# Low parts of 22 weight blocks: a GpSimd subtraction, or an accumulating DMA onto a negated copy

## The chip, the core and the metric

The kernel runs on one core of a Trainium2 chip. The metric is the device time of one execution in microseconds (us). TensorE (PE, with its weight loads PEld) does the matrix products, VectorE (DVE), ScalarE (ACT) and GpSimd (POOL) the rest; SyncE (SP) issues the DMAs of the kernel before. Line numbers such as L427 are those of the kernel's file; since every instruction is issued from one line of a recording helper, the names of tiles tell instructions apart.

## The reference

One decoder layer over x of 1024 tokens by 1024 channels, in float32, with a modulation vector c:

```python
mod = silu(c) @ w_mod + b_mod                    # sh1, sc1, g1, sh2, sc2, g2
h = rms_norm(x, norm_mix_w) * (1 + sc1) + sh1
proj = h @ w_in                                  # 1024 x 3080
x_lru, y_lru, qkv, z, beta, alpha = split(proj)  # 512, 512, 3 x 512, 512, 4, 4
out_lru = rms_norm(rg_lru(conv(x_lru), ...) * gelu(y_lru), lru_norm_w)
q, k, v = silu(conv(qkv))                        # 4 heads of 128
o = gated_delta_rule_chunked(q, k, v, g, beta)
out_gdn = rms_norm(o, gdn_norm_w) * silu(z)
x = x + g1 * (concat(out_lru, out_gdn) @ w_out)
h = rms_norm(x, norm_mlp_w) * (1 + sc2) + sh2
x = x + g2 * (square(relu(h @ w_up)) @ w_down)
out = rms_norm(x, final_norm_w)
```

The delta rule needs, for each chunk of a head, the inverse of a triangular matrix made from k, beta and g.

## The kernel before

**Two parts for each operand.** A product in float32 is made of three products in the faster type fp32r: an operand is split into a high part (the value rounded to fp32r) and a low part (the value minus the high part), and `mm3` adds high x high, high x low and low x high in one PSUM bank. Its third matmul is the one that reads the low part of the weights.

**The input projection.** `w_in` is worked off in 24 blocks of 128 columns (`Proj`): k0 to k3, z0 to z3, then q and v of each of four heads in turn, then lx and ly of four channel tiles in turn. `Proj.split` loads a block of 1024 x 128 as a tile of 128 x 1024 (512 KB), casts it on ScalarE to its high part (`k_wh`, `z_wh` and so on) and subtracts to get its low part (`k_wl`, `z_wl`). For k0 and k1 the subtraction is on VectorE, for the other 22 blocks on GpSimd. `Proj.third` makes the product for 342 of the columns of h at a time (the last two of 1026 carry a bias): 8 x 3 matmuls of 342 columns, so 72 for a block. ScalarE then evicts the three results (`k_st`, `z_st`).

**What hangs on a block.** `key(h)` takes a projected k through a convolution and silu (`k2T`, `k3T`: one ScalarE multiplication, three VectorE steps, one ScalarE tanh `k2th`, `k3th`, one VectorE step), transposes it on TensorE (`ktok`), multiplies it with itself (`kk`), scales with `rnk` (a power on GpSimd), `bcoef` and the decay (`k_dm`) and writes `LT`. After k3, `inverse` runs a long row of small VectorE steps (`ftmp`, `xx`), transposes the result (`xnc`, `xtc`), copies it to `xn` and `xt`, and multiplies on TensorE (`ie`, `ig`, `ih`, `ix`). Then come query, value and the chain over the chunks (`ch`), the RG-LRU (`lru`), the output projection (`wg`, `wl`), and the MLP as a seven-product Strassen scheme (`upx`, `upy`, `upz`, `dn`).

**The order.** Nothing is issued while the kernel is written down. A `Recorder` collects every operation with a planned duration, and `schedule` simulates the five engines and puts their instructions in an order that is then fixed. The large products are a backbone (`bb`) with due times from a backward pass; other operations get the due time of what needs them, moved by one entry of the table `SHIFTS` for each operation. On an engine, a ready side operation goes ahead of the backbone. The backward pass is

```python
for op in reversed(ops):
    op.lst = min((ops[j].lst - lat(op, ops[j]) for j in op.succs), default=0.0) - op.dur * scale(op)
```

Large tiles, the raw block and both of its parts among them, share a pool of 43 buffers; a buffer comes free when the last operation that uses its tile has ended. The planner lets only one of GpSimd and some VectorE instructions run at a time (`port`).

Of the kernel before, what the change touches and what calls it, by code (L numbers as in the profile page):

```python
# [51 lines left out]
LOAD_WINDOW, DUE = 40.0, 5.0  # L52
RESERVE = {"b": 11, "ps": 2, "u": 1, "c": 2}
# [67 lines left out]
def dram_box(ap):  # L121
# [7 lines left out]
    'c-qaId2m(NeaC<AJ?ZI5LLdnV0RkZwiG4R<wm^)7YrMprIwncm)J@}Qn;B2s&a}-;-8P+MlCeAWA6YtW)=nmlGmY(z3C0fC21AT77@NiHn8ip4f%'  # L129
    'X-NC;j^Qo%_IG`(AS%vFr1jyS#hvx%Zsk`7Phy@0^#`w7v|jSNWjw&9C+Kw%f@gO~HjJheRg#*x5f{vi-x<OUf<RRC=f{IG#@j$BiBGF_eaG+uxu'  # L130
    '0_O5~3b>G0Eo_FtW8hH2o?GNZ}bLLu6`uV|I2Oq!m-usK({d=@J9o>#ro%nn2TN|U~Tjz`hBr-xS>2PV$J)AF+Cp1UWdXn=AvOzcNo4S+p<+4r>>'
    'JBZW=2VGGLP|vScKMQ|ptuytP<iOeyG!JI@<94#*(2j*TY9S``wv_^qcQ2=dxP4?`w|%*$N08LF27ZW(gu-Q$&nr{<=Z<{KGCHgZWuq-$QNZmUx5'
    'c>>3N9^anz>?dL=SODr7p8lqK>xxHO<m@}~UTd)}p2`uZeWySBrDv~H1IaQ?JTme0sy$<Mtd_p$h9_+xZJFKLHX@XadOEL-Gv@`ko(z0Tr`9eT-|'
    'cSor4XrfN5V>!~K)ux~NliYl%=KJkh<oeWsZ1n3{MzJ2cpc_*!Cvs%Cl*&jcW-Qmnb|)su&GhEH7Sr$JT1k&9C11u%4Zn@XaMq|J<Q<*HHk!@1rI'
    'qxwRR`$%zc&6%zI0(jU4DJlz}4eY%rke$47n94Kcq*IxM?z5=DE=+N5X_(CdKW%C8#q<or&xR>8b6FVw^Q;5{<2+$31YjO;78AETpnL_o#QR@!nt'
    'Q)^42{uZG8QYWHg#&CHcv#_S&Sdba$D%;H|I6lC<R2dj~$P9@S*A#;$?2iT8fw5s6Wbe^tdtmZIc(>b%+2{_uVWpWCB_Aqvpa#-hiw{s#gwNlE@`'
    'qgUDb)G!@Pd%r3GFzwWEBcRm99#CfdqV@VYvbFFlrN`mWyo$L<D7&?v(dEAprc8+P|B8%jKtWRv=zx*s9$@L{B68*DEt++el@v@!|4u3J=f47-Ks'
    'C>(>lt1B`8DC+NA8%X7r#6%A*~(@V$x93N-yLEX5l66fG-*!#i)#4i>Pj&TMPg9*|!k5#Qnb5p2>^Tz`V?VaDX!+?^w%XwfKISS|DE^DLPxeR|nS'
    'T~8Tw{Z6A>X?i#SHF8ZeT4nNM?;nX}DCM1bP?1M(hC9lpd<}XU64{Pjt&=v+_R3G>Tk<co=iBl_`0)s5tB`_G@1t>!mNP!99NmuePj)mP9<7zn%A'
    'K;1^F`2DSs?duoQn^gBa>u3GUQ*1y=(MlfdX#IQmS4;vOgX_o5xoFv3#rB`zwLO$E3@<rs=(JX;=RmlR;Sh;DJhxLmbXftXmw*lFvRLlu?ddk2!z'  # L140
    'PPhXlq9)noMGBnh;tU!}jde>_Dy^QT5S%wDA$MY?A`a1;6JOrPgkh6HgVyJ*Vn#Vh=$8@hYfN|^Ta~IT)jf(O7B`pwtO|_96^zOrq8`6k?;%pPKq'
    'NSPN1GK+|{^a3Z&S@t-9n5HHuWm;Mj>CyI&6m%EX*TI=YB9~DVllu9d0g+sBitcV<iB(V=;#}|R$tYx>oa<CFb-$x^@y4TT~eb)e5*LW5cq}`H8O'
    '-BT)E7}BxiMS`?&rVOEbk?>GS5*7)Sp2+_y#&?wB;@aBjXoh)|j|#n#|R9HxKQ7sVW<z(++$!91wS`OjI5%V#+o&lpwEk^otnt;nG#39jXUMDwXt'
    '!d3&#1OeP8ce5?xdBfWYFurdOEHa3DbLyww-`Ni@{z8U1gxm}sDnh~(Evf_26w3u&jCXw7#W0HG+yh$7rT0tOa*_OTaBL>g!BTY6Xt;FhDJ)beR;'
    'K{2-6h|UAK*b%S2?8Gr?qb1rnfjAp3pBMwS~kED;TqRvOG2lsoH^bzk}=-$fx1pEN53@a5;xjZ3VCW2T{qdiC$XuCF<rn{qg73AUbx3cdb@$4yTD'
    'o&eP&^IvxobCWfO5ke!mN#=2WCG7cuErlEyARVbsO5l|Vwn&Cz-*HtT=Or_vP%=Ozlg5hm(Nq^*Cm?#%n=%%k{>HBo9SZq0(Z6<9fC$?NbuRq18j'
    '{%DfMbFOZGWHgoKC4?8<>Oeb9=$jApzPA;^ygTr(Xv&)A`c>U+x0~!bK^ncH-X$lw$P)a$mBLQqs<(@!tt5RZ?k7#kO0ZYi5vzv#^8kgE_YJ)XW;'
    'a&y9j?6^j)}nj0mAiE$4NY8^@T#;InC=$&Iyi8rm@zYdDpw6KH)GeeKGEx975`<3EO_$W{)$G;i_8Qt0>+lwq9pX+Wj$B*m2qIM9bj?MF6~V#k6^'
    'b|atbCeb6rte|BX-cWzPS?n~>w~WFj`PC@G`o=)?DP%9@`f60-EWJgLUzXPyxeG2+l9D}eBF3GQ`f#k$dEXR0Ol3ysIlVkm2Q~1N_Qo={B@Q*+iN'
    'zARHxr+&0maOx?ouRnDPLR)eV*e3Y+sg}h$t>P*}I$8CD4OD{WS7a$-9=I_bai7_u@qk;H9li1M1uJo6wI6Zw}XZ*RVLd-(?{EN~g}wB9`(+9ix!'  # L150
# [23 lines left out]
    '#<|Y#)#B?c5?`E!oYgx7T_D*+2DaLyl5J!bU%pKyyA@ld;;&bOaKYyHS|W2BVKGWl#!IKur;ju1Q0lC95_!n;u3P4^bmOu4e-5w5Va;qdvl02&s}'
    '&&a!}x|%>OTWB#H|)G?{*ws`txHi(L}r2+*`E_Wbyw#TZNT$`SPS27vFOE|0_E)|K`YMTukn>%~o{L`;9~wo6yf4H~3$`Gg+)MvXyJ*opRjF_io*'
    ')+w_gA;)Lrhdo-Y}VAcb=J&P42bBKedIeazR*=)b^j2ebor_bwhEUv%3T+R2(@iHaI;Uu?S%~u9enYHfaj{ZMN;)>r-WKnmlL#x5wsL0Xit0?#%k'
    'd?`qE7_GJE>H1{K8|1Vt-DjdhlCwvoR59NbHwk@78Yeut6fhz#NVC;&bI%<*i6JJ9qRqvAg&DJ_UUXRu&s;m8@6V1j@#SO(3u?rX{g9rBCahqM=$'
    '|y#qce@C5TbaYc^}%>#uOy-;X4(p~WC&qvddCnEQ|6WeWZs?7xb%BJ*bBOL@fnV7MGLWpX=p;PIbju{yd8|I(-p*cQtl`qrP4q1r2F{|BmuXWI')
SHIFTS = array.array("h", zlib.decompress(base64.b85decode(_SHIFTS))) if _SHIFTS else None
# [1500 lines left out]
```

## Time and profile before

| | us |
|---|---|
| median of 3 runs | 1164.97 (1164.01 to 1165.21) |
| profiled execution, first to last instruction (span) | 1162.6 |
| what lies around the span, against the median | 2.4 |
| PE busy | 1137.1 |
| POOL busy | 371.4, 221 instructions |
| ACT busy | 616.5 |
| DVE busy | 834.6 |

The record of the profiled execution gives its span; its time is compared with the median through the 2.4 us of the third row. Busy time is the union of an engine's instructions. A matmul is pipelined: its row gives some 320 ns for a 342-column one, though in an unbroken row the next one starts earlier. In a timeline a line has the start, the length, the engine, operation and tiles, and in brackets how long the engine stood idle before it and what ended that. A row of a group has busy time, the mean of one in ns, and the idle time before, with its releasers.

### The profile page before, as it was taken

What the parts mean: (1) busy time and instruction counts of PE and PEld (TensorE: products, weight loads), DVE (VectorE), ACT (ScalarE), POOL (GpSimd) and SP (SyncE); (2) the same over time, 40 slices, a digit from 0 to 9 for tenths busy, and PEclk for the clock granted to TensorE, in tenths of its full rate; (3) what the DMA queues carried; (4) which work ended last, traced back from release to release, by engine and by line L of the source; (5) the groups of instructions that cost most, each with busy time, mean ns of one, the idle gap of its engine ahead of it and who ended that gap; (6) DMA issues with size and microseconds to landing.
All of it is one profiled execution on the core that took longest, in us unless ns stands there. A gap on an engine that the chain in (4) does not pass through costs nothing.

```text
span 1162.6 us, 15986 instructions
## 1 busy us (share of the span) xinstructions
PE 1137.1 (98%) x5952; PEld 979.8 (84%) x5952; DVE 834.6 (72%) x1123; ACT 616.5 (53%) x988; POOL 371.4 (32%) x221
## 2 busy tenths in 40 slices
PE   6899999999999999999999999999999999999997
PEld 3799999999999998887888888887888888888885
DVE  5778786687986879778776776766885583865563
ACT  5547445445547866477655555556644533363441
POOL 1329512253424463300003231311450057723030
PEclk9999999999999999999999999999999999999999
DMA  9623432544454462422276887773999956864541
GB/s 338 223 86 110 134 121 75 180 121 159 152 185 145 135 230 107 145 84 80 65 267 237 274 281 247 252 244 136 364 403 388 369 175 247 308 226 168 199 163 72
DMA packets 127151, 229.52 MB, mean 197 GB/s; under 512 B 10657, under 2 KB 51806, under 8 KB 127074
## 3 DMA queue, kind: packets, MB, share of 16 engines
q1 hardware_dynamic: 127074, 228.51, 56.7%
q8 instruction: 46, 0.75, 0.3%
q14 instruction: 31, 0.25, 0.1%
HBM read 171.83 MB, written 56.65 MB: 197 GB/s over the span
## 4 chain that ended last, share of the span: by engine, by line
PE 91%; DMA 3%; DVE 3%; ACT 1%; issue 1%; SPq 1%; POOL 0%; POOLq 0%; ACTq 0%
PE dn L427 26%; PE upx L427 15%; PE upz L427 8%; PE wg L427 4%; PE upy L427 4%; PE wl L427 4%; PE z_p L427 4%; PE lx_p L427 4%; PE q_p L427 4%; PE ly_p L427 4%; PE v_p L427 3%; PE k_p L427 2%; PE ch L427 2%; SPq L427 1%; DMA sh_w<-in_w_mod_dram 1%
## 5 line engine op out<-in xcount | busy, mean ns | idle before, releaser
L427 PE MATMUL upx<-h2h,U 128*128 128x512 f32 x512 | 168.0, 394 | 0.0
L427 POOL TENSOR_TENSOR wd<-wd,wd 128x512 f32<-128x512 f32 x32 | 49.9, 1568 | 214.4 <-DMA wd<-in_w_down_dram 163.4
L427 PEld LDWEIGHTS upx<-h2h,U 128*128 128x128 f32 x512 | 96.0, 188 | 22.5
L427 PE MATMUL upx<-h2l,U 128*128 128x512 f32 x256 | 100.8, 394 | 0.0
L427 DVE TENSOR_TENSOR U<-wu,U 128x512 fp32r<-128x512 f32 x112 | 85.0, 774 | 18.1 <-ACT U L427 17.9
L427 ACT ACTIVATE act<-act 128x512 f32<-128x512 f32 x112 | 70.3, 632 | 44.9 <-DVE act L427 43.2
L427 PE MATMUL upz<-h2h,U 128*128 128x512 f32 x256 | 85.0, 394 | 0.0
L427 ACT CAST U<-wu 128x512 fp32r<-128x512 f32 x112 | 66.8, 617 | 27.8 <-DVE wu L427 10.0
L427 PEld LDWEIGHTS upx<-h2l,U 128*128 128x128 f32 x256 | 48.1, 188 | 11.5
L427 PEld LDWEIGHTS upz<-h2h,U 128*128 128x128 f32 x256 | 48.1, 188 | 11.4
L427 DVE TENSOR_TENSOR act<-upz,ek 128x512 f32<-128x512 f32 x32 | 22.1, 690 | 40.1 <-PE upz L427 25.9
L427 ACT COPY ek<-upx 128x512 f32<-128x512 f32 x48 | 28.0, 584 | 42.6 <-PE upx L427 42.4
L427 PE MATMUL upz<-h2l,U 128*128 128x512 f32 x128 | 50.4, 394 | 0.0
L427 POOL TENSOR_TENSOR R<-R,R_5o 128x1024 f32<-128x1024 f32 x8 | 20.0, 2520 | 74.4 <-DMA R<-in_w_down_dram 63.2
L427 PE MATMUL upy<-h2h,U 128*128 128x512 f32 x128 | 42.7, 394 | 0.0
L427 POOL TENSOR_TENSOR ssq<-ssq,mhalf 128x1 f32<-128x1 f32 x16 | 11.6, 725 | 84.8 <-DVE ssq L427 84.8
L427 DVE TENSOR_TENSOR wu<-wu,wu 128x512 f32<-128x512 f32 x48 | 36.1, 759 | 0.5 <-DMA wu<-in_w_up_dram 0.4
L427 ACT ACTIVATE vn<-ch,bcoef 128x128 f32<-128x128 f32 x32 | 11.8, 368 | 45.0 <-PE ch L427 44.9
L427 PE MATMUL k_p<-hh,k_wh 128*128 128x342 f32 x96 | 31.9, 332 | 1.0 <-ACT hh L427 1.0
L427 PE MATMUL k_p<-hl,k_wh 128*128 128x342 f32 x96 | 32.0, 333 | 0.8 <-DVE hl L427 0.8
L427 PE MATMUL k_p<-hh,k_wl 128*128 128x342 f32 x96 | 31.9, 332 | 0.0
L427 PE MATMUL ly_p<-hh,ly_wh 128*128 128x342 f32 x96 | 31.7, 330 | 0.0
(574 smaller groups left out, 3719.3 us busy)
## 6 DMA issues: line engine op xcount, KB each, us to landing
L<-aod SPq DMA_DIRECT2D x56, 512.0 KB, 6.5
R<-in_w_down_dram SPq DMA_DIRECT2D x40, 512.0 KB, 5.9
wu<-in_w_up_dram SPq DMA_DIRECT2D x32, 512.0 KB, 5.0
aod<-as SPq DMA_DIRECT2D x64, 256.0 KB, 3.3
wd<-in_w_down_dram SPq DMA_DIRECT2D x32, 512.0 KB, 6.5
aod<-act SPq DMA_DIRECT2D x48, 256.0 KB, 2.9
x<-in_x_dram SPq DMA_DIRECT2D x16, 512.0 KB, 4.6
sc_w<-in_w_mod_dram SPq DMA_DIRECT2D x16, 512.0 KB, 7.2
```

The source lines that it names most:

```text
L427: op.fn(*[res(v) for v in op.a], **{n: res(v) for n, v in op.k.items()})
```

## The change

For the 22 blocks, ScalarE writes the negated high part into the low part's tile, and a DMA issued by GpSimd adds the raw block to it in place. The planner learns of such an operation: 1.1 us of GpSimd, and a landing time after it that delays those who need the result. `SHIFTS` is another table, so the order of instructions differs on all engines. k0 and k1 keep their subtraction on VectorE.

```diff
+ADD_ISSUE, ADD_LAND, ADD_RATE = 1.1, 2.5, 150e3
...
 _SHIFTS = (
...
-        op.adj = SHIFTS[len(self.ops)] / 4.0 if SHIFTS else 0.0
+        op.adj = SHIFTS[len(self.ops)] / 4.0 if SHIFTS and len(self.ops) < len(SHIFTS) else 0.0
...
                 now[e] = fin = t + (clock.run(t, op.dur, op.work) if e == "PE" else op.dur)
                 port = max(port, fin) if op.port else port
+                fin += op.tail
...
+class Adder(Proxy):
+    def __getattr__(self, name):
+        fn = getattr(self.nce, name)
+
+        def call(out, in_):
+            n = 4
+            for d in out.shape:
+                n *= d
+            self.rec.add("POOL", fn, (), {"out": out, "in_": in_, "accum_op": ALU.add}, [out], [in_, out], ADD_ISSUE)
+            self.rec.ops[-1].tail = ADD_LAND + n / ADD_RATE
+        return call
...
+    GD = Adder(rec, "POOL", nc.gpsimd)
...
             A.copy(self.w[0], raw)
-            e.tensor_tensor(out=self.w[1], in0=raw, in1=self.w[0].bitcast(F32), op=ALU.subtract)
+            if e is G:
+                A.mul(self.w[1], self.w[0].bitcast(F32), -1.0)
+                GD.dma_start(out=self.w[1].bitcast(F32), in_=raw)
+            else:
+                e.tensor_tensor(out=self.w[1], in0=raw, in1=self.w[0].bitcast(F32), op=ALU.subtract)
```

More of the change, by code (lines that the diff above doesn't have):

```diff
@@ L134 @@
[L134 to L138, printed above, removed]
@@ L174 @@
[L174 to L178, printed above, removed]
+    'c-qZd2XIy8x?SHsCkc?y5(q><AoQk4ODNI}AXS<mNQ)v$lPW|EO%PDQ!j(`(lxE@5L<FvaC`~|0gosojNJ2t@bdsF!u6?*O_stvsGqW>qoVPP4=Vb5wx'
@@ new lines @@
+    '38>kt$&|XhoG9LvhGm))iHN`ZuUL<!@`t@Cu*MuYGv7<V)N|ZGc;Q#=}L|NAMIbwefXZ7|L}d!ef$l_pPBaWVgDKX=YlSJrXV8gzt{H`{P**vzgTVRf6'
+    'f)p-|gw>S)cd6uSa;V_tGl)zUNUMBmU3V_JZfW$7!2z{G{Qip`|ermvyi1)C^sKE?9tBSfbOg5%KyJ@^qQrMxf+rHyw)~wUgXMUmUb%y3e}?Nrc2=wJT'
+    'Qq(aJi3auRHPCM!{0YKljP=Xb{jl$4S(8)Z;ml0DZ8N@1Gz&{FtR1F%}>X;19bdwNBC>KYxTA7Bzf&|B})k`=A`IHLG}ew49_Ksn3BNJBT-hVQW&FUcL'
+    'Nwlqdd3`0F$U5$ZqU;R;AB5@jFvIP@l5yokvZh}AR>La+RG5V6eg|4y!pUd-zlc9LZO4Wf#L@=h%CI^v(9D3+HuIYBIAV26$6$D|IK8h_`4Mk}25E-cj'
+    '`aaJW!ABb9*mlR*;t%$jhAdA$BjK!W&|v>${YWdp#jCIANZv6)&w5_x7|D#5C*X$w&g%*~NHlJtEN2JQKqMNV1j^xUJdIVdQuat4v_XHlEX(DZOhzoGv'
@@ new lines @@
+    ';B77`#@FKI*#05^pMuX&ukyZxT(z5PEU;X=Ijp5(F1x~lhp-}rg((5%i#H7apAmrbO0uzKjxtwLZvz0!}B<-osp=4II0tA>#MpFosg*~*}gfEZ!6yi75'
+    'u2sg}BX3N!8i9ME5ziZ8mLm$8mK1?s%NCIHlj}B-;LS4dwh(^&93_hQ7;dop21lc=P@_#37F>KEeo%l1<F-3t9sAG*i>`HqRboq;)_(^Yo-VkeZCiHF9'
+    '1oS}TY>Dz@unscL0uG>XX%&C<pg<#?ukjEw><d(&B~@3GzCNC!2aEfNsp`An<mc|EGPbS^sMJ4ST?(zOnIoPuwdiDgh(M&pDQ!zk30T&aj(HH`ON(XSX'
+    'uZ|EZC*-p4zi4tK&%W=G+!_W->VlM2|K^!R#hqSI0g|Y182IKl3d$O}CU(=aGi5i54=!JM}!%OVPA9>cxG70lh&gFKsmIV6aG;?SzvWTCz(a(Agw5zMX'
+    '>vg}`@|8QnHNa}&e#Zhlvd6v5s%Gu-J1Z@%J613My0Q+hN?ER=Gu(2Ak-9{JF@q7eULY%E2xg)MF?<p4=!P*;456sRJoUpER-=K$mJ6Imj`nAky735V$'
@@ new lines @@
+    'vG6m0_lT_Qbkz#<ftBy_ZT<d$qCL*F&vZ8MFQ|AvoMUgTwXdd)9$fa)RrJLVyiqIiaj!h+4mY!QB|U?X08}%W}T5<oNaN8vPyBZ8m>4@bv3h=xGq?wtW'
+    '8!Es|PE`61gi=q?;A)3a33=Ta)n&^S6Yo;;j1Nxa88KgYlJ=B)a~}DC~#H>c(@@0fDS#?c@=z23+$BnMYeUm&p=?O+>|MT=8D|KT(r7OJE2dM^z-_b;+'
+    'b%pLV&h)tc&_?~Zq`*B7h?uHCLUo?nEanBvaS{iw}RXZ!V&`Br~-2frB1#ru}J@A##;)7%TK40nC@*UcS*N)nD<er1?J{qQoHN;g+2WNEH8!ZODg(5Ns'
+    '>$8k1JAzGF}6{KlL$D>(=sM9XTqu40^r$)&J;*Qg{(ab#ONb2<XoZc7aY!PfPgwL`auj;Pj7WcI{k~B&05c>*<`oLp+2Xnp=8Jz9Ok*I)DL_!bI%B~U|'
+    'g?SCs#il}Vu?~#=KODDv(eXH4$g|#)L99>qTw4;8ddLB^k)BeSxObYIY?tIokZYH?v5bfqX1!s(gR0gLNws3JR%TnbaoH6ve#F5*w6s1%0X~(d@F*>FO'
@@ new lines @@
+    'UF2#&pooev5s49a@<0-Hfz{OR+TfFpkK4n9MXnpO+UI=%a)QE{)*Aoi?RT{tTm{~>>kh04RD6MGFhk6JCkr7-_k+{i2co($MHn-TI8s`UF*?T%Ak(U;+'
+    'bc42*z4*WU8aAy&Ow09t|YQ^{vjAqGVEi$>^@4Ek4m;DUU~G3X%2<Iao{Dt|>mW*@otEW*%0(_gIn3;x*QfcUWl-lW|;N40d+BcDt(2`5SO2jxn$f^=Z'
+    '>zv<B<XeOlRtH5$olZE*rknDHsN$hzL1TBxWbB0*+Z4PD3ON%<%1tUoKxan|A2WV-}QTgJr<Z>A-2<##kdQZ<CNVJvcWF#TDB*>{;(_cU2rAfClHdY^T'
+    'pD7nE@{Ri3oPukwQa%V?<_WbAHprtCaz8)gCf0O>6gR)jW+0|*u(9y(`ClTP9z?uw9lSNXX3GzUrMdV9)R=$>WR>}ulV>2@I3)qYvwCfMrj@9#D<O-*?'
+    'h(sWU3}ynOwK<y7BC+Vs=wWr%Y~85qtVkJ;wfZ(0{xaI|eRBNG(un-Uj;vdHh|JZ^*BhMSR(+0mR*9N-m}HSHr0W9e*lzLz(fd_es(`&axA97P@NLHyJ'
@@ L179 @@
+    '%TlkW&>Rb_zYvHB?dcgzn8DF(m+q?2UZv&tz7&Y99Ay)'
+)
 SHIFTS = array.array("h", zlib.decompress(base64.b85decode(_SHIFTS))) if _SHIFTS else None
@@ L204 @@
     __slots__ = ("adj", "work", "port", "eng", "fn", "a", "k", "outs", "ins", "dur", "bb", "preds", "succs", "allocs", "bufs", "lst", "ready",
-                 "need", "load", "bias", "pri", "tiny")
+                 "need", "load", "bias", "pri", "tiny", "tail")
 class Recorder:
```

81 lines of the change are left out of this document (41 added, 40 removed).

## The prediction

> **What bounds the kernel now.** I read the page's busy shares and its chain first, then the stages, to see where TensorE has any time to give.
>
> ```profile
> span 1162.6 us, 15986 instructions
> PE 1137.1 (98%) x5952; PEld 979.8 (84%) x5952; DVE 834.6 (72%) x1123; ACT 616.5 (53%) x988; POOL 371.4 (32%) x221
> PE 91%; DMA 3%; DVE 3%; ACT 1%; issue 1%; SPq 1%; POOL 0%; POOLq 0%; ACTq 0%
> ```
>
> TensorE is busy for 98% of the span and is 91% of the chain that ended last; GpSimd, which the change relieves, is busy for 32% and is 0% of it. The stages (stretch, its length, then PE, PEld, DVE, ACT, POOL busy, granted clock, DMA share, GB/s) say where the missing 25.5 us are:
>
> ```profile
> 0.00:50.00 50.00, 36.32 (x179) 24.52 (x180) 29.90 (x62) 30.16 (x47) 10.25 (x19) 0.97 0.90 312
> 50.00:100.00 50.00, 49.28 (x330) 45.80 (x329) 39.72 (x92) 28.18 (x73) 22.96 (x12) 1.00 0.33 107
> 100.00:150.00 50.00, 49.06 (x327) 48.77 (x326) 40.73 (x79) 21.28 (x40) 30.75 (x33) 1.00 0.32 106
> 150.00:200.00 50.00, 50.00 (x402) 50.00 (x401) 37.71 (x72) 28.11 (x54) 10.06 (x5) 1.00 0.33 107
> 550.00:600.00 50.00, 50.00 (x217) 40.46 (x216) 38.55 (x55) 32.68 (x53) 0.00 (x0) 1.00 0.41 141
> 1100.00:1163.00 63.00, 54.96 (x238) 44.20 (x236) 27.90 (x37) 20.52 (x32) 13.04 (x12) 0.97 0.32 118
> ```
>
> 13.7 us are idle in the first 50, where the two blocks that the change leaves alone run, 8.0 in the last 63; the stages with the 22 blocks (50 to about 425) have next to nothing: 0.7, 0.9 and 0.0 in the three shown. So there is little to win there, and since a stage such as 550:600 has no idle time at all, whatever TensorE loses before it is not caught up later.
>
> Why there is no idle time, although the decay and inverse work of the keys is a long chain on VectorE and ScalarE, the chain of waits shows (start, length, what):
>
> ```profile
> 98.49 2.77 DVE k2T L427
> 102.45 1.17 DVE k2T L427
> 103.67 1.09 PE ktok L427 x8
> 104.76 1.79 PE kk L427 x16
> 106.55 9.89 PE z_p L427 x63
> 116.44 1.11 PE kk L427 x10
> ...
> 119.58 33.12 PE z_p L427 x211
> 152.70 11.26 PE q_p L427 x72
> 163.96 2.21 PE v_p L427 x14
> 166.16 1.79 PE ie L427 x16
> ```
>
> While VectorE makes k2T and k3T, TensorE is filled with the projections z0 and after them z1 to q0 and 14 matmuls of v0. One such matmul takes 9.89/63 = 0.157 us. The filling works because z0's low part is ready 30 us early:
>
> ```profile
> 65.02 1.03 ACT L427 CAST z_wh<-z_w 128x1024 fp32r<-128x1024 f32 x1
> 66.13 2.38 POOL L427 TENSOR_TENSOR z_wl<-z_w,z_wh 128x1024 fp32r<-128x1024 f32 x1 [11.21 <-ACT z_wh L427]
> 100.85 0.32 PE L427 MATMUL z_p<-hh,z_wh 128*128 128x342 f32 x1
> ```
>
> **The change part by part.** *Removed:* 22 GpSimd subtractions.
>
> ```profile
> L427 POOL TENSOR_TENSOR lx_wl<-lx_w,lx_wh 128x1024 fp32r<-128x1024 f32 x4 | 11.6, 2892 | 26.0 <-ACT lx_wh L427 26.0
> L427 POOL TENSOR_TENSOR z_wl<-z_w,z_wh 128x1024 fp32r<-128x1024 f32 x4 | 9.7, 2440 | 11.2 <-ACT z_wh L427 11.2
> ```
>
> At 2.44 to 2.89 us that is 54 to 64 us of GpSimd, on an engine with 0% of the chain: worth nothing by itself. It also frees VectorE, which is held up where both want operands:
>
> ```profile
> 143.20 2.56 DVE L427 TENSOR_TENSOR xx<-xx,ftmp 128x255 f32<-128x255 f32 x1
> 145.79 0.43 DVE L427 TENSOR_TENSOR ftmp<-gg,xx 128x256 f32<-128x256 f32 x1
> 154.40 2.46 DVE L427 TENSOR_TENSOR ftmp<-gg,xx 128x156 f32<-128x156 f32 x1
> 156.89 0.32 DVE L427 TENSOR_TENSOR xx<-xx,ftmp 128x156 f32<-128x156 f32 x1
> 143.03 2.44 POOL L427 TENSOR_TENSOR q_wl<-q_w,q_wh 128x1024 fp32r<-128x1024 f32 x1 [10.45 <-ACT q_wh L427]
> 154.29 2.39 POOL L427 TENSOR_TENSOR v_wl<-v_w,v_wh 128x1024 fp32r<-128x1024 f32 x1 [8.81 <-ACT v_wh L427]
> ```
>
> Each of these two subtractions makes one small step of the inverse take 2.1 us more. Without them the inverse is ready 4.2 us earlier. TensorE did not wait for it, so this too is no gain by itself, but it lowers a loss below.
>
> *Added:* 22 negating copies on ScalarE. As a cast of the same tile they cost 1.03 us, 22.7 us in all; ScalarE is busy for 21 to 28 us of each 50 in the stages shown, so its sum has room, and only the copies that stand ahead of an urgent instruction count. Added, too, are 22 accumulating DMAs of 512 KB on GpSimd's queue. No row shows one. The nearest are plain transfers of the same size:
>
> ```profile
> kd<-ktail SPq DMA_DIRECT2D x4, 512.0 KB, 2.9
> z_w<-in_w_in_dram SPq DMA_DIRECT2D x4, 512.0 KB, 5.0
> wo<-in_w_out_dram SPq DMA_DIRECT2D x8, 512.0 KB, 7.2
> ```
>
> From below 2.9 us for a plain store. From above 14.4 us, twice the slowest, since an accumulation reads its destination as well. I take 6 us from issue to landing: twice the store (5.8), and near the loads at the same DMA share (5.0). The Trainium skill, page "DMA: Bandwidth & Descriptors", section "Anatomy of one DMA", gives a DMA issued by GpSimd about 2.0 us and its bytes at 436 GB/s, which for 512 KB would be an estimate of 3.2 us. The store's 2.9 agrees for a plain copy; no run here shows it for an accumulation. By that rule the sum below would stay and rival (a) below would be out, its chance going to the forecast. SP's queue loses nothing and gains nothing; a raw block is held some 3 us longer, with 43 buffers.
>
> *Moved:* the order of the built program differs on every engine, and here the cost lies. Counted in both programs: ahead of the first ktok of k2 stand 11 matmuls of z0 before and 2 after; ahead of the first kk of k3 stand 74 z matmuls before and 26 after, with the same number of all others; ahead of the first ie stand 288 z, 72 q and 14 v before, and 288 z and 24 q after. The reason is in ScalarE's list: z0's cast still comes early, but its negation comes 28 rows later, behind k2th and an eviction of k3, and the DMA stands on GpSimd behind the second rnk:
>
> ```profile
> 101.29 1.06 ACT L427 ACTIVATE k2th<-k2T 128x1024 f32<-128x1024 f32 x1 [0.95 <-DVE k2T L427]
> 103.34 0.55 ACT L427 ACTIVATE k_st<-k_p,k_b 128x342 f32<-128x342 f32 x1
> 104.61 1.15 ACT L427 ACTIVATE k3T<-k_st,cols 128x1024 f32<-128x1024 f32 x1
> 100.14 2.63 POOL L427 TENSOR_TENSOR rnk<-ssk,mhalf 128x8 f32<-128x8 f32 x1
> 114.31 1.23 DVE L427 SCALAR_TENSOR_TENSOR k3T<-k3th,k3T 128x1024 f32<-128x1024 f32 x1 [1.45 <-ACT k3th L427]
> ```
>
> The planner's backward pass for due times takes off an operation's own duration and not the new landing time, so copies and DMAs come just in time. With the rows: k2th ends at 102.35, an eviction (0.55) and the negation (1.03) end near 103.9, GpSimd is free since 102.77, the DMA lands at 103.9 + 6 = 109.9. TensorE does two z0 matmuls from 100.85, waits for k2T (103.6), does its 16 or so short ones to 106.5, and waits for z0's low part, its third operand, until 109.9. Then 24 matmuls (3.8 us) bring it to 113.7, and it waits for k3T, which was ready at 115.54. The three waits together are what the counts say: 48 fewer z matmuls done when k3's kk starts at 116.44, 48 x 0.157 = 7.5 us lost. The landing has 2.7 us to spare in this (116.44 - 113.7). The negation of z0 stands on ScalarE ahead of the k3T multiplication at 104.61, and z1's ahead of k3th: I add 1.0 us for one of them. Bounds: 5.5 if k3T comes 2 us sooner, since VectorE's order changed too; 9.5 if both negations count.
>
> At ie TensorE has done 62 fewer (62 x 0.157 = 9.7 us); with the inverse 4.2 us sooner this asks for a loss of only 5.5, less than it has by then, so nothing is added.
>
> The other 19 blocks: z3 and q0 are cast and negated behind the last eviction of the block before the one being projected. A block is 72 matmuls, 11.3 us; less an eviction (0.55), cast and negation (2.1) and hand-overs, some 8.4 us are left for issue and landing. At 6 us and 1 for the issue they fit. By the same count in the built order some nine blocks are this tight (z0 to z3, q0, v2, q3, v3, lx0); the rest have more.
>
> The sum: 1162.6 + 7.5 + 1.0 = 1171.1 of span. The median shown is 1164.97, 2.4 above this span, for what lies around it; so **1173.5 us**.
>
> **The rivals.** (a) *The landing is slow.* An accumulation that takes 11 us with its issue overruns 8.4 by 2.6 at nine blocks: 23 us more, 1197. For it: nobody waits for less than the whole transfer, and the bound from above is 14.4. Against it: the DMA share of these stages is 0.32. It decides from 8.4 us on. (b) *The relief wins, faster.* VectorE no longer meets 22 subtractions, 2.1 us each, TensorE waits for nothing, and the idle time of 50 to 150 goes: 50 - 49.28 and 50 - 49.06, 1.7 us off the median, 1163.3, which is faster. It decides if z0's low part lands by 102, which needs the negation before k2th, and it stands behind it. The Trainium skill, "SBUF — State Buffer", section "Who interferes with whom", says a VectorE instruction with two SBUF inputs contends with a GpSimd one that reads SBUF; the rows at 143.20 and 154.40 agree. By that rule alone, without the order, the time would be this one. (c) *No change.* k3T comes so much sooner without contention that kk of k3 starts at 109 and nothing is lost: 1165. The rows speak against it: between 69 and 115 no removed subtraction runs, so VectorE's contended steps there (k2T 2.77) are with others that stay.
>
> **How the numbers follow.** The forecast case (a loss of 3 to 16 us, 1168 to 1181) gets 0.67, (a) 0.20 between 1181 and 1210, (b) 0.06, (c) 0.07. About 0.2% (2.3 us) is what a measurement can tell. Range: from 1167.5, below the forecast's lower bound, to 1192, so that the worst third of (a), (b) and (c) are left out, 0.07 + 0.06 + 0.07. Faster 0.06, same 0.07, slower 0.67 + 0.20 = 0.87.
>
> **What would show it.** In the new profile: waits of PE for the DMA into z_wl and for k2T and k3T between 100 and 120, 7 to 9 us together; POOL busy lower by 54 to 64 us less what its DMAs show; PE at 50.00 of 50 from 550 on, as before. Landings of the new DMAs near 6 us. I am wrong if PE idles less than 3 us between 95 and 120, or if waits for low parts recur block after block.

## The result, and the profile after

The changed kernel takes 1184.28 us (median of 4 runs, 1183.57 to 1186.23), the kernel before on the same chip 1165.09 (4 runs, 1164.01 to 1166.00): a ratio of 1.0166, 95% interval 1.0152 to 1.0180. It is slower by 19.2 us. That lies in the predicted range (1167.5 to 1192); the forecast itself, 1173.5, had 8.5 us, less than half of the loss. The profiled execution has a span of 1182.8 us, 20.2 above the one before.

The page of the changed kernel, its span, busy shares and the shares of the chain:

```profile
span 1182.8 us, 16057 instructions
PE 1145.3 (97%) x5952; PEld 985.6 (83%) x5952; DVE 828.1 (70%) x1123; ACT 634.3 (54%) x1010; POOL 333.8 (28%) x221
PE 90%; DVE 4%; DMA 3%; issue 1%; SPq 1%; ACT 1%; POOLq 0%; POOL 0%; ACTq 0%; DVEq 0%
```

GpSimd is relieved of 37.6 us (it still issues 22 DMAs of 0.88 each, 19.4, so the subtractions were some 57) and VectorE of 6.5, ScalarE has 17.8 more. TensorE idles 37.5 us (25.5 before) and is busy 8.2 us longer, with the same 5952 matmuls. Its stages (stretch, length, PE, PEld, DVE, ACT, POOL busy, granted clock, DMA share, GB/s):

```profile
100.00:150.00 50.00, 43.23 (x250) 42.45 (x250) 33.47 (x73) 26.66 (x52) 24.85 (x31) 0.86 0.59 162
150.00:200.00 50.00, 50.00 (x393) 49.83 (x392) 27.32 (x66) 28.60 (x55) 4.14 (x3) 1.00 0.44 122
280.00:345.00 65.00, 60.73 (x439) 59.27 (x438) 55.95 (x76) 35.11 (x59) 16.34 (x9) 1.00 0.73 223
700.00:750.00 50.00, 48.54 (x209) 38.91 (x208) 35.65 (x47) 24.86 (x45) 9.18 (x6) 1.00 0.74 249
```

The last two of these stages in the kernel before:

```profile
280.00:345.00 65.00, 64.09 (x464) 63.35 (x464) 57.32 (x81) 32.24 (x57) 20.55 (x8) 1.00 0.58 196
700.00:750.00 50.00, 50.00 (x217) 40.40 (x216) 36.64 (x52) 25.22 (x45) 8.56 (x6) 1.00 0.70 233
```

Two things stand in the first row of the changed kernel: 6.8 us without work, about the forecast's 7 to 9, and a granted clock of 0.86, which was 1.00 before. Closer, in windows of 4 us, and TensorE's own rows (start, length, what, [idle before, released by]):

```profile
98.00:102.00 4.00, 3.38 (x22) 3.10 (x20) 4.00 (x6) 2.79 (x8) 2.16 (x5) 1.00 0.69 216
102.00:106.00 4.00, 1.61 (x8) 1.61 (x9) 1.62 (x5) 3.74 (x7) 2.90 (x3) 0.69 0.79 264
106.00:110.00 4.00, 4.00 (x19) 3.79 (x19) 2.09 (x4) 2.01 (x3) 3.92 (x2) 0.50 0.78 175
114.00:118.00 4.00, 0.24 (x2) 0.19 (x2) 2.88 (x8) 3.36 (x7) 3.69 (x3) 0.90 0.01 2
118.00:122.00 4.00, 4.00 (x19) 4.00 (x20) 0.79 (x3) 0.93 (x2) 4.00 (x4) 0.50 0.34 133
122.00:126.00 4.00, 4.00 (x23) 4.00 (x23) 3.15 (x6) 1.28 (x4) 0.91 (x2) 0.75 1.05 243
```

```profile
101.06 0.32 PE L443 MATMUL z_p<-hl,z_wh 128*128 128x342 f32 x1
104.39 0.69 PE L443 MATMUL ktok<-ident,k2T 128*128 128x128 f32 x2 [3.01 <-DVE k2T L443]
104.87 1.91 PE L443 MATMUL kk<-k2T 128*128 128x128 f32 x8
109.69 0.65 PE L443 MATMUL z_p<-hh,z_wl 128*128 128x342 f32 x1
113.73 0.32 PE L443 MATMUL z_p<-hl,z_wh 128*128 128x342 f32 x1
117.81 0.80 PE L443 MATMUL kk<-k3T 128*128 128x128 f32 x2 [3.76 <-DVE k3T L443]
```

After two z matmuls TensorE waits 3.0 us for k2T, and after 24 more 3.8 us for k3T. Behind each wait its clock is halved: a kk matmul takes 1.91/8 = 0.24 us (before, 1.79/16 = 0.11). The granted-clock records put the half clock at 103.55 to 110.38 and at 117.21 to 124.03, twice 6.83 us; before there was none between 47 and 1159. The first begins while TensorE still waits: by then it had been idle 2.2 of the last 3.4 us. The matmul of z0's low part starts at 109.69, right behind the landing of its DMA, which was issued at 104.76 and landed at 109.65. The trace counts no idle time ahead of it, because the 24 short matmuls of k2 ran at half clock until then. q0's DMA landed as narrowly, at 165.04 for a matmul at 165.08. No accumulating DMA kept TensorE idle. The view of the transfers (KB, median us from issue to landing):

```profile
z_wl<-z_w POOLq DMA_DIRECT2D x4, 512.0 KB, 5.6
q_wl<-q_w POOLq DMA_DIRECT2D x4, 512.0 KB, 6.8
v_wl<-v_w POOLq DMA_DIRECT2D x4, 512.0 KB, 7.7
lx_wl<-lx_w POOLq DMA_DIRECT2D x4, 512.0 KB, 6.7
ly_wl<-ly_w POOLq DMA_DIRECT2D x4, 512.0 KB, 4.5
```

These are medians; the single ones lie between 4.4 and 10.9 us.

Further on, VectorE's and GpSimd's rows, and the TensorE rows that wait for them, show a second kind of loss:

```profile
293.52 3.29 DVE L443 SCALAR_TENSOR_TENSOR v2T<-v2th,v2T 128x1024 f32<-128x1024 f32 x1
333.83 4.82 DVE L443 SCALAR_TENSOR_TENSOR v3T<-v3th,v3T 128x1024 f32<-128x1024 f32 x1
293.33 2.40 POOL L443 TENSOR_TENSOR kTl<-kTl,q_gb 128x1024 f32<-128x1024 f32 x1 [17.09 <-PE qk L443]
332.52 2.70 POOL L443 TENSOR_TENSOR q3T<-q3T,q_gb 128x1024 f32<-128x1024 f32 x1
334.88 2.67 POOL L443 TENSOR_TENSOR kTl<-kTl,q_gb 128x1024 f32<-128x1024 f32 x1
296.95 0.41 PE L443 MATMUL vtok<-ident,v2T 128*128 128x128 f32 x2 [1.22 <-DVE v2T L443]
338.79 0.41 PE L443 MATMUL vtok<-ident,v3T 128*128 128x128 f32 x2 [1.31 <-DVE v3T L443]
```

These GpSimd multiplications are not among the 22 that went. In the new order they run beside the last step of v2T and v3T, which takes 1.2 us when undisturbed and here 3.3 and 4.8. Each of the two ends 1.1 us behind the last GpSimd row beside it (295.73 and 337.55). The order before had kTl and q3T beside earlier steps of v2T and v3T, and TensorE waited for neither:

```profile
277.47 3.00 DVE L427 SCALAR_TENSOR_TENSOR v2T<-v_st,cols,v2T 128x1024 f32<-128x1024 f32 x1
320.82 2.84 DVE L427 SCALAR_TENSOR_TENSOR v3T<-v_st,cols,v3T 128x1024 f32<-128x1024 f32 x1
```

To see where the 20.2 us are lost I price each matmul at its form's usual spacing in the kernel before (0.157 us for a 342-column one) and compare when two traces have done the same amount of work. The lag behind the kernel before, at that kernel's times, for this trace and those of the experiments (e1 is the first experiment below, and so on; e4 without its added work):

```
at, us                           55    90   125   160   270   345   480   560   750    end
after                          -0.8   0.1  12.2  12.4  12.5  16.5  15.9  17.8  19.6   20.2
e1  before's order, DMA        -0.2   1.4   4.5   5.1   8.4  13.0  14.0  14.0  13.9   14.3
e2  after's order, subtraction  0.4   7.7  18.7  26.2  26.6  31.5  31.1  32.8  34.3   34.7
e3  z0 early                    0.4   1.9  11.9  17.8  38.0  43.7  43.1  45.0  46.0   46.3
e4  fill at k3                  0.8   0.8   9.7  14.1  14.2  17.2  16.5  18.3  19.0   19.6
e5  hybrid                      1.5   1.5   1.4   1.4   3.1   5.0   6.2   6.3   6.0    6.5
e6  four steps on VectorE       0.5   1.8  13.7  15.6  15.7  16.3  15.5  17.4  19.3   20.1
e7  before, no table            6.1   8.7  14.8  14.8  25.5  25.2  29.0  29.7  29.6   29.5
e8  after, no table            -0.3  -0.6   6.4   7.5   7.8   6.6   7.0   8.6   8.3    8.2
e9  landing in the due times    1.1   0.6   3.5   7.7   9.3  11.9  13.3  14.1  13.8   14.1
e10 new order                  -0.8  -1.2  -1.9   1.5   2.8   8.9   8.5   9.2   9.0    9.0
e11 constants alone             0.1  -0.3   0.8   7.4   8.1   9.0   8.6  10.8  10.7   10.7
e12 new order, two subtracted   0.0  -0.5  -1.1  -1.1   1.4   1.8   1.7   2.4   2.3    2.5
```

Each line is one execution. The first accumulating DMA is issued near 50, so what stands at 55, up to 1.5 us either way in all but e7, is mostly how that execution started.

For the changed kernel: 12.1 us at k2 and k3 (5.8 more idle; 13.7 us at half clock, 1.4 of them idle, so 6.1 lost), 4.0 where v2T and v3T are late, 1.9 from 480 to 560 (0.9 of it longer waits for h2r, the rest not traced), 1.8 by 750 (one wait of 1.5 for U). The 19 other blocks between them cost nothing.

### The profile page after: what moved, and what is told of

Read it like the earlier page. It is cut to its first block, busy times and chain, and to the rows that moved or that the text cites. A ratio compares the mean times of both kernels' runs of the same rounds, so it can differ in the third digit from the quotient of the medians.

```text
span 1182.8 us, 16057 instructions
## 1 busy us (share of the span) xinstructions
PE 1145.3 (97%) x5952; PEld 985.6 (83%) x5952; DVE 828.1 (70%) x1123; ACT 634.3 (54%) x1010; POOL 333.8 (28%) x221
## 4 chain that ended last, share of the span: by engine, by line
PE 90%; DVE 4%; DMA 3%; issue 1%; SPq 1%; ACT 1%; POOLq 0%; POOL 0%; ACTq 0%; DVEq 0%
PE dn L443 26%; PE upx L443 15%; PE upz L443 8%; PE ly_p L443 4%; PE wg L443 4%; PE wl L443 4%; PE upy L443 4%; PE q_p L443 4%; PE lx_p L443 4%; PE z_p L443 4%; PE v_p L443 3%; PE k_p L443 3%; PE ch L443 1%; PE cho L443 1%; SPq L443 1%
## 5 line engine op out<-in xcount | busy, mean ns | idle before, releaser
L443 PEld LDWEIGHTS upx<-h2l,U 128*128 128x128 f32 x256 | 48.1, 188 | 11.5 <-issue 0.2
L443 DVE TENSOR_TENSOR wu<-wu,wu 128x512 f32<-128x512 f32 x48 | 40.0, 842 | 3.5 <-DMA wu<-in_w_up_dram 3.4
L443 POOL TENSOR_TENSOR ssq<-ssq,mhalf 128x1 f32<-128x1 f32 x16 | 12.1, 759 | 74.9 <-DVE ssq L443 74.8
L443 PE MATMUL v_p<-hh,v_wh 128*128 128x342 f32 x96 | 31.9, 332 | 0.0
L443 PE MATMUL v_p<-hh,v_wl 128*128 128x342 f32 x96 | 31.6, 329 | 0.0
```

What stands on the lines that cost most here:

```text
L443: op.fn(*[res(v) for v in op.a], **{n: res(v) for n, v in op.k.items()})
```

## The experiments

The theory: the loss is the order in which the instructions now stand, not the DMA. Against it stood the landing, the traffic of 22 more transfers, and ScalarE's copies.

**Before's order with the DMA.** In the kernel before, where the schedule is issued:

```diff
+            if i in self.low:
+                self.nc.scalar.mul(wl, wh, -1.0)
+                self.nc.gpsimd.dma_start(out=wl.bitcast(F32), in_=raw, accum_op=ALU.add)
+                continue
             op.fn(*[res(v) for v in op.a], **{n: res(v) for n, v in op.k.items()})
```

> The order of the kernel before, with its table; only at the place of each of the 22 GpSimd subtractions now stand the negating copy on ScalarE and the accumulating DMA. Theory (the DMA itself is harmless where the order leaves it time, and the loss of the changed kernel lies in its order): the filling at k2 and k3 stays as before (11 and 74 z matmuls ahead of them), so the half-clock periods near 104 and 117 are gone. But four subtractions of the kernel before start only 2.8, 4.0, 4.3 and 6.5 us ahead of the first matmul that reads them (z1, z2, v2, lx0), and a negation and a landing of 5.6 to 7.7 us behind its issue take 7 to 9: waits of TensorE for these low parts, 4.5 + 3.5 + 4 + 2 = 14 us, about 1179 (1173 to 1186). Rival one (the transfers cost by themselves wherever they stand): more than that, above 1186, with waits at more than these four blocks. Rival two (the relief of GpSimd and VectorE wins where the order is kept): 1165 or below.

Measured 1178.97 us (1177.61 to 1183.24), ratio 1.0136 (1.0110 to 1.0162). TensorE's timeline has four waits for low parts:

```profile
122.87 0.42 PE L433 MATMUL z_p<-hh,z_wl 128*128 128x342 f32 x1 [2.29 <-DMA z_wl<-z_w]
170.20 0.42 PE L433 MATMUL v_p<-hh,v_wl 128*128 128x342 f32 x1 [0.80 <-DMA v_wl<-v_w]
260.25 0.42 PE L433 MATMUL v_p<-hh,v_wl 128*128 128x342 f32 x1 [1.91 <-DMA v_wl<-v_w]
316.63 0.42 PE L433 MATMUL lx_p<-hh,lx_wl 128*128 128x342 f32 x1 [1.67 <-DMA lx_wl<-lx_w]
```

They are z1, v0, v2 and lx0. z2 was expected and waits 0.3 us only; v0, with 9.8 us, was not. Together they are 6.7 us, not 14, so the total came out right for partly wrong reasons: the rest is a half-clock window behind lx0's wait and longer waits for k2T (1.5 us, 0.9 before), r, S and xrh. From 90 to 125, z1's wait included, the lag grows by 3.1 us, not 12.1. An order made for a 2.4 us subtraction does not suit a DMA that lands in 4.4 to 9.5.

**After's order with the subtraction.** In the changed kernel the copies are left out and a GpSimd subtraction is issued where the DMA stood:

```diff
+            if i in self.skip:        # the copies
+                continue
+            if i in self.low:
+                self.nc.gpsimd.tensor_tensor(out=wl, in0=raw, in1=wh, op=ALU.subtract)
+                continue
```

> The order of the changed kernel, with its table; only the 22 negating copies are left out and a GpSimd subtraction stands at the place of each accumulating DMA. Theory (the order is the loss): 1184 again, 1180 to 1188, with waits of about 3 and 3.8 us for k2T and k3T and the two half-clock periods behind them; ScalarE's 22 copies less may take some 2 us off. Rival (the DMA's landing or its traffic is the loss): back to 1165 to 1170.

Measured 1198.57 us (1195.82 to 1201.69), ratio 1.0296 (1.0274 to 1.0318): outside both expectations. The lag table takes it apart. At k2 and k3 it loses 11.0 us (the changed kernel 12.1), from 270 to 345 4.9 (4.0), from 480 to 560 1.7 (1.9), from 560 to 750 1.5 (1.8): without a single accumulating DMA the order loses about as much in the same stretches. What it loses beyond that, 7.6 us more by 90 and 7.3 more from 125 to 160, are subtractions that meet VectorE, seen on TensorE as

```profile
62.14 3.54 PE L450 MATMUL sh_c<-ones,sh_acc 128*128 128x1 f32 x16 [3.14 <-DVE sh_acc L450]
180.71 6.58 PE L450 MATMUL ie<-xn,LT 128*128 128x128 f32 x42 [5.50 <-ACT xn L450]
```

VectorE's busy time is 861.1 us here and 828.1 with the DMA. So copy and DMA in place of the subtraction are a gain in this order, of 1198.57 - 1184.28 = 14.3 us. Both orders with both operations:

| | subtraction | copy and DMA |
|---|---|---|
| before's order | 1165.09 | 1178.97 |
| after's order | 1198.57 | 1184.28 |

In each order the operation that it was made for is the better one, by some 14 us. With the DMA in both, the order made for it is the worse one by 5.3 us; with the subtraction in both, by 33.5. So the places at which the changed kernel loses its time are the order's; that the DMA is free wherever it stands is not shown, and in before's order it is not.

**z0 early.**

```diff
                 GD.dma_start(out=self.w[1].bitcast(F32), in_=raw)
+                if self.name in ("z0",):
+                    rec.ops[-1].bias = rec.ops[-2].bias = -30.0
```

> The changed kernel; only z0's negation and DMA are made due 30 us earlier, and the planner orders anew: 26 z matmuls stand ahead of k2's first and 74 ahead of k3's first (2 and 26 in the changed kernel). Theory (TensorE without filling at k2 and k3, and the half clock that follows these waits, cost 12.3 of the 19 us): no half clock between 100 and 125, 1184.3 - 12.3 = 1172, 1168 to 1178 since the rest of the order changes too. Rival (the landing or contention with the 22 DMAs is spread over the stages): 1180 to 1185.

Measured 1211.63 us (1210.00 to 1212.58), ratio 1.0406 (1.0390 to 1.0421): both expectations missed. At k2 the theory's part came true, with a lag of 1.7 us at 110. But the planner's new order has the same kind of gap further on:

```profile
121.38 0.42 PE L443 MATMUL z_p<-hh,z_wh 128*128 128x342 f32 x1 [3.54 <-ACT z_wh L443]
129.21 0.42 PE L443 MATMUL z_p<-hh,z_wl 128*128 128x342 f32 x1 [2.96 <-DMA z_wl<-z_w]
169.36 6.78 PE L443 MATMUL ie<-xn,LT 128*128 128x128 f32 x44 [4.04 <-ACT xn L443]
```

z0 is used up, z1 is not there, and from 242 to 268 of this trace the recurrence runs with one projection matmul beside it (the lag grows by 20 us from 160 to 270). Moving one block made a new order everywhere, so this tests the whole order, not the block.

**Matmuls to keep the clock up.**

```diff
+            if op.eng == "PE":
+                for nm, cnt in (("k3T", 22),):
+                    if nm not in self.seen and any(b.name == nm for b in op.bufs):
+                        self.seen.add(nm)
+                        pk = op.a[0].buf.get()
+                        for _ in range(cnt):
+                            op_mm = self.nc.tensor.matmul
+                            op_mm(pk[:, 0:342], self.h0.real()[:, 0:P], self.h0.real()[:, 0:342], start=True, stop=True)
```

> The changed kernel with 22 more matmuls of 0.157 us, 3.5 us of them, ahead of k3's first use, written into the kk tile that is overwritten right behind them: nothing is added to the result, and they stand in the 3.8 us in which TensorE waits for k3T. Theory (the half clock from 117.2 to 124.0 follows from the idle window ahead of it and costs half of what runs in it): the granted clock stays at 1.00 there, and 6.2 us of work at half clock take 3.1: 1184.3 - 3.1 = 1181.2, 1180 to 1182.5. Rival (TensorE would wait for something else anyway, so the clock there costs nothing): 1184.3 +- 0.8. The first half-clock period, near 104, stays, and lies ahead of the wait for k3T, which hides it.

Measured 1187.55 us (1184.03 to 1190.57), ratio 1.0199 (1.0175 to 1.0223): no gain, as the rival says, but the median lies 2.5 us above the rival's range too, and why is open; the profiled execution is the fastest of the four, 1184.03. The clock did stay at 1.00 behind k3T, and by 125 TensorE was 2.5 us better off than in the changed kernel (a lag of 9.7). It lost 4.4 where the inverse is waited for, with a half-clock window of its own there:

```profile
168.62 6.55 PE L452 MATMUL ie<-xn,LT 128*128 128x128 f32 x42 [2.38 <-ACT xn L452]
```

The half clock behind k3T is a loss only as far as nothing behind it waits anyway. The next bound, the inverse, lay less than 3 us off.

At k2 the same trace settles something else. The half clock there lasted 3.41 us, not 6.83, TensorE had its short matmuls done sooner, and now it does wait for z0's low part:

```profile
110.32 0.42 PE L452 MATMUL z_p<-hh,z_wl 128*128 128x342 f32 x1 [0.77 <-DMA z_wl<-z_w]
```

So the first half clock of the changed kernel costs nothing by itself: it fills the time until z0's DMA lands.

**Hybrid.** The first experiment's kernel, with the subtraction kept for the tight blocks:

```diff
-            if e is G:
+            if e is G and self.name not in ("z1", "z2", "v2", "lx0"):
                 rec.low.append(len(rec.ops) - 1)
```

> The order of the kernel before, with the copy and the accumulating DMA at the place of 18 of the subtractions; the four that stood within 6.5 us of their first use (z1, z2, v2, lx0) stay GpSimd subtractions. With the DMA at all 22 the same order took 1179.0, with 6.7 us of TensorE waits for low parts (2.29, 0.80, 1.91, 1.67) and a half-clock window behind the last. Theory (a DMA with 9 us of time or more ahead of its reader costs nothing): the four waits and the half clock go, and what hangs on them, 1164 to 1169. Rival (ScalarE's 22 more copies ahead of urgent steps are the other half of that loss: k2T 1.5, ch 1.3, gate 1.4 us): 1169 to 1173.

Measured 1170.49 us (1168.05 to 1171.19), ratio 1.0035 (1.0022 to 1.0047): in the rival's range. 8.5 us of the 14 are gone with four of 22 DMAs. But the rival's account fits only in part: the wait for k2T is 0.9 us, as in the kernel before. Of this trace's 6.5 us, 1.5 stand there by 55, where a half-clock window of the start falls later than in the kernel before, at 51.34 and not 42.88. A wait of 1.57 is for v0's DMA, though the subtraction there had stood 9.8 us ahead of its reader: the theory's 9 us were too few. The rest is mostly longer waits for r (1.3, 0.7 before), S (0.8, none before) and xrh (1.4, 0.5 before), all of the first experiment too. That these come from ScalarE's copies is argued from their place, not shown.

**Four GpSimd steps on VectorE.**

```diff
+            if i in self.onv:      # kTl2, q3_dm, kTl3, q3T
+                self.nc.vector.tensor_tensor(**{n: res(v) for n, v in op.k.items()})
+                continue
```

> The changed kernel with four GpSimd multiplications and additions (kTl and q_dm of heads 2 and 3, q3T) done by VectorE, behind the urgent step they ran beside. In the trace of the changed kernel v2T's last step takes 3.29 us, a step of sc_acc 3.47 and v3T's last step 4.82 beside them, 1.2 to 1.3 elsewhere. Theory (the loss of 4 us between 285 and 320 is this meeting of GpSimd and VectorE, which the new order brought about): these steps take 1.2 to 1.3, and TensorE's waits behind them (1.2 + 1.3 + 0.5 + 1.0) go: 1184.3 - 4.0 = 1180.3, 1179 to 1182.5. Rival (those waits are of the transfers or of ScalarE): 1184.3 +- 0.8, and TensorE waits at the same places.

Measured 1184.64 us (1178.78 to 1188.20), ratio 1.0153 (1.0125 to 1.0181): no gain in the median. At its place the theory holds in full:

```profile
296.69 1.22 DVE L462 SCALAR_TENSOR_TENSOR v2T<-v2th,v2T 128x1024 f32<-128x1024 f32 x1
334.90 1.22 DVE L462 SCALAR_TENSOR_TENSOR v3T<-v3th,v3T 128x1024 f32<-128x1024 f32 x1
280.00:345.00 65.00, 64.25 (x465) 62.88 (x464) 55.95 (x84) 38.27 (x65) 6.85 (x5) 1.00 0.72 226
```

1.22 us each, and TensorE idles 65 - 64.25 = 0.75 us from 280 to 345, where the changed kernel has 65 - 60.73 = 4.27; from 270 to 345 the lag grows by 0.6, not 4.0. But this trace was 3.2 us further behind at 270, ahead of the edit, where both kernels have the same instructions in the same order: 1.3 at the start, and a wait of 1.6 for xn that the changed kernel's trace does not have. The runs of this kernel lie 9 us apart. Whether that is the half clock's windows falling differently on the same waits is open.

**No table, before and after.** In both kernels:

```diff
-_SHIFTS = ('...')
+_SHIFTS = ''
```

> The kernel before with an empty table of shifts: the planner orders by its own rules alone. To be compared with the changed kernel without its table, in the same call. Theory (the DMA relieves VectorE by itself, and the changed kernel loses only because its order fits worse than the one before): without tables the changed kernel is the faster of the two, by 5 to 25 us. Rival (the copies and the DMAs cost by themselves): the kernel before is faster without tables too, by 10 to 20 us. The level of both is not known; above 1165 for this one.

> The changed kernel with an empty table of shifts. Theory: 5 to 25 us faster than the kernel before without a table, and near the changed kernel with its table (1184.3), since that table leaves the gaps at k2 and k3 (here 31 and 74 z matmuls stand ahead of them, with the table 2 and 26). Rival: 10 to 20 us slower than the kernel before without a table.

Measured 1189.72 us for the kernel before (1187.74 to 1193.90; ratio 1.0210, 1.0192 to 1.0228) and 1172.75 for the changed kernel (1172.58 to 1173.19; 1.0060, 1.0046 to 1.0074). Without tables the change is a gain of 17.0 us, as the theory says, though the second kernel is not near 1184.3, as it also said, but 11.5 below. The table of the kernel before is worth 24.6 us to it; that of the changed kernel costs it 11.5. VectorE's busy time is 840.1 us in the first and 812.9 in the second, and by 90, where subtractions meet VectorE in the first, the two are already 9.3 apart. It is one pair of orders; other planner rules could give another difference. What is left of the loss in the second is again at k2 and k3, 7.0 us with the half clock (0.6 ahead by 90, 6.4 behind at 125):

```profile
108.74 1.97 PE L380 MATMUL ktok<-ident,k2T 128*128 128x128 f32 x8 [3.42 <-DVE k2T L380]
122.56 1.09 PE L380 MATMUL ktok<-ident,k3T 128*128 128x128 f32 x8 [1.53 <-DVE k3T L380]
```

**The landing in the due times.** The kernel without a table, and:

```diff
-            ... default=0.0) - op.dur * scale(op)
+            ... default=0.0) - op.dur * scale(op) - 1 * op.tail
```

> The changed kernel without its table, and the planner's backward pass takes off the landing of a DMA as it does an operation's duration, so that copies and DMAs come due earlier; 87 z matmuls now stand ahead of k2's first matmul and 103 ahead of k3's (31 and 74 without the landing in the due times, 1172.75). Theory (what is left of the loss is TensorE without filling at k2 and k3, 7 us of the 8.3 against the kernel before, and it comes from due times that leave out the landing): 1172.75 - 5 to 7 = 1166 to 1168, with full clock from 90 to 130. Rival (the filling is only taken from where it is wanted later, ahead of the inverse's matmuls): 1171 to 1175, with a wait for xn before ie.

Measured 1178.03 us (1176.77 to 1179.35), ratio 1.0108 (1.0095 to 1.0121): neither. The gap at k2 went, the one at k3 stayed (2.1 us), a z block's DMA is now waited for (2.4 us at 136), and vn 2.6 us at 317. The reason that the prediction gave for the late low parts is right as a reading of the planner; mending it alone makes the time worse.

**A new order.** As the last, with three constants and 22 groups shifted; and the constants alone:

```diff
-SIDE_SCALE = 1.4
+SIDE_SCALE = 1.5
-SLACK, SLACK_TINY = 0.3, 2.0
-LOAD_WINDOW, DUE = 40.0, 5.0
+SLACK, SLACK_TINY = 0.2, 3.0
+LOAD_WINDOW, DUE = 38.0, 5.0
...
+for _a, _b, _d in [(1181, 1211, -16), (4764, 4794, -16), ...]:   # not in the second kernel
+    for _i in range(_a, _b):
+        SHIFTS[_i] += _d
```

> As the kernel with the landing in the due times, with three of the planner's constants changed (side work 1.5 long, not 1.4; slack 0.2 and 3.0, not 0.3 and 2.0; loads 38 us ahead, not 40) and 22 groups of operations shifted by 1 to 8 us: 74 z matmuls ahead of k2's first, 101 ahead of k3's. Theory (with an order made for it the accumulating DMA is no loss, and its relief of VectorE is left as a gain): below the kernel before, 1156 to 1164. Rival (the change costs 5 us or more in any order): 1168 or above.

> As the kernel with the new order, without the 22 shifts: landing in the due times and the three constants. Theory: between the two others of this call, 1160 to 1168. Rival: 1168 or above, as there.

Measured 1173.65 us (1168.08 to 1175.43; ratio 1.0061, 1.0042 to 1.0081) and 1174.69 (1173.18 to 1175.37; 1.0077, 1.0064 to 1.0090): the rivals' side. The 22 shifts are worth 1 us, less than the spread of the runs. Yet up to 125 the new order is 1.9 us ahead of the kernel before. It then loses 3.4 us by 160 and 6.1 from 270 to 345, at two places:

```profile
131.66 0.42 PE L383 MATMUL z_p<-hh,z_wl 128*128 128x342 f32 x1 [3.13 <-DMA z_wl<-z_w]
...
303.75 2.67 POOL L383 TENSOR_TENSOR q_dm<-q_gb,neg 128x1024 f32<-128x1024 f32 x1 [7.42 <-DMA q_gb<-gdr]
...
308.04 0.80 PE L383 MATMUL ch<-vn,ktl 128*128 128x128 f32 x2 [2.71 <-ACT vn L383]
```

The first is the landing of an accumulating DMA. In the second a load of q_gb comes late, q_dm's rows on ScalarE behind it hold up vn, and a half-clock period follows.

**The new order, two blocks subtracted.** z2 and lx0 of the new order as in the second experiment:

```diff
+                if self.name in ("z2", "lx0"):
+                    rec.low[len(rec.ops) - 1] = (self.w[1], raw, self.w[0].bitcast(F32))
```

> The new order (1173.65), with a GpSimd subtraction in place of copy and accumulating DMA at two blocks only, z2 and lx0. In the trace of the new order TensorE loses 4.0 us near 131, where it waits 3.1 us for z2's DMA (issued 7.8 us earlier, behind other work of GpSimd), and 6.4 near 300, where a load of q_gb of head 3, issued 0.5 us ahead of lx0's DMA, lands 8.8 us later, q_dm's work holds up ScalarE, and a half-clock period falls there. Theory (what is left of the loss in this order is the landing where little time is left for it, and its traffic): both go, 1173.65 - 10 = 1163.5, 1161 to 1166, below the kernel before. Rival one (q_gb is late by itself, the DMA beside it has no part): only the first goes, 1169 to 1171. Rival two (the subtractions bring back their meeting with VectorE): 1172 or above.

Measured 1169.21 us (1166.17 to 1170.95), ratio 1.0032 (1.0020 to 1.0043): better by 4.4, at the foot of the first rival's range by the time. The trace sides with the theory in that both losses are gone; the lag is 2.5 at the end. q_gb, issued at 293.34, is in use at 299.02, after 5.7 us and not 8.8. That lx0's DMA had delayed it is not shown: kTl's load stands 2.5 us ahead of it here and 1.6 before, and in the hybrid the same load landed only after 8.8 us with no accumulating DMA under way.

```profile
293.34 0.33 SPq L390 DMA_DIRECT2D q_gb<-gdr  x1
299.02 2.40 POOL L390 TENSOR_TENSOR q_dm<-q_gb,neg 128x1024 f32<-128x1024 f32 x1 [3.52 <-DMA q_gb<-gdr]
```

This profiled execution took 1166.88 us, near the lowest; why the others take up to 4 us more stays open. No version with the accumulating DMA was faster than the kernel before. Whether one would be with a table tuned for it as well as the kernel before's is for its own is not tested.

## Why the prediction was half right

The sum had one loss, 7.5 + 1.0 us at k2 and k3. Two terms that it put at nothing failed it: the clock behind the wait for k3T, 3.1 us, and everything behind ie, 7.7 us.

*The order is where the cost lies*: right for the places. The order alone loses in the same stretches without any DMA (second experiment), and the DMA in before's order loses elsewhere (first), but there it costs 13.9 us too.

*8.5 us at k2 and k3*: the term that was mis-sized; 12.1 measured. The counts were right: up to k3's first kk, 48 z matmuls fewer (7.5 us) and a start at 117.81 in place of 116.44 (1.4) make 8.9. What was left out is the clock: behind the wait for k3T it is halved, and (6.83 - 0.60)/2 = 3.1 us more are lost there. The row of the first 50 us had 0.97 for a clock, and I did not ask what a new wait of 3 us would do to it. The Trainium skill, "TensorE: Matmul & The Clock Gate", section "Part 1: The HAM clock gate (the "warmup" mystery)", gives half rate after an idle window of about 3.4 us, free-running. The trace agrees on windows of 3.41 us; but 2.2 us idle in one of them was enough.

*Waits for z0's low part until 109.9*: right in time, hidden in the trace. The DMA landed at 109.65 and z0 went on at 109.69; the prediction's 24 matmuls then end near 113.7, as it said. But TensorE was not idle for it: it had been doing k2's short matmuls (24, not "16 or so") at half clock. Where the half clock was shorter the wait shows (0.77 us, fourth experiment). That the idle time of 6.8 us comes near the "7 to 9 us" is partly luck, since one of the three waits in it was replaced by the clock. Rival (a), the slow landing, did not happen in this order: the slowest took 10.9 us, for v1, which was read 28 us after its issue.

*Nothing added at ie, inverse 4.2 us earlier*: no loss there, as said, but ie starts at 168.63, not earlier than before's 166.00. The row of small steps of the inverse is 3.2 us shorter, not 4.2 (25.0 us from 135.98, 28.2 from 131.84), and it starts 4.1 us later, because k3's work came later.

*The other 19 blocks fit*: right, no idle time for a low part, but with luck at q0: it had 8.64 us and needed 8.60. Rival (c), k3's kk at 109 and nothing lost, is out: it starts at 117.81.

*PE at 50.00 of 50 from 550 on, nothing else lost*: the step that failed. I compared the two orders only at k2, k3 and ie, and took the rest as before. 7.7 us lie behind: 4.0 by GpSimd work that stayed and now meets urgent VectorE steps (shown at its place by the sixth experiment), 1.9 at h2T and 1.8 at U. The second experiment loses 1.7 and 1.5 in these last two stretches, so they go with the order; what in it makes them has no experiment of its own.

*The range*: that 1184.28 lies in it is luck. It is outside the forecast case's own bounds (1168 to 1181), and the part above them stood there for a slow landing, which did not happen.

*Rival (b), the relief wins*: not against the kernel before, but within after's order by 14.3 us, and without tables by 17.0. The Trainium skill, "SBUF — State Buffer", section "Who interferes with whom", says that a VectorE instruction with two SBUF inputs contends with a GpSimd one that reads SBUF. 861.1 against 828.1 us of VectorE in one order agree. What decides this comparison is that one table is worth 24.6 us to its kernel and the other costs its kernel 11.5.

## What to carry to other kernels

In a kernel planned as a whole, a change of one operation is a change of the order: compare the two orders on every engine and along the whole program, and try both kernels without their tuned tables before the change itself is judged. A wait of 3 us on TensorE is to be priced with the half clock that may follow it, and then checked against what waits next: at k2 the half clock only filled the time until a DMA landed, and behind k3T its price could not be won back. An operation is to be judged in both orders: here each was 14 us better than the other in its own. An accumulating DMA in place of a subtraction frees VectorE, but it needed up to 11 us ahead of its reader (v0: 9.8 of them and a wait of 0.8 to 1.6), and is better left out where there is less.

## What was not expected of the hardware

TensorE's clock halved after a window of 3.41 us in which it worked 1.2 us and idled 2.2. In each trace the half-clock periods begin whole multiples of 3.41 us apart, and behind a single wait they last one such window or two. Over the traces from 95 to 320 us (without the third experiment's from 240 on, where short waits follow one another) there are 21: 3.41 us in all 11 cases where TensorE was at work again when the period began, 6.83 in all 10 where it still waited then. So the same wait of 3.01 us for k2T was followed by 6.83 us in the changed kernel and by 3.41 in the fourth experiment, and a wait of 3.13 us that fell into two windows (the new order, at 131) by none.

An accumulating DMA of 512 KB issued by GpSimd landed in 4.5 to 7.7 us (medians by tile in the changed kernel; single ones 4.4 to 10.9). A VectorE step with two inputs beside GpSimd multiplications took 3.3 to 4.8 us, not 1.2: it ended 1.1 us behind the end of the last of them, as if it had begun only then.
